# Modulation of two adaptive-norm layers: row sums of products on VectorE, in place of matmuls with the condition as weights

## The chip, the cores and the metric

The kernel runs on one core of a Trainium2 chip. The metric is the device time of one execution in microseconds (us). TensorE does the matrix products and writes them to PSUM, VectorE (DVE) and ScalarE (ACT) do the elementwise work, GpSimd (POOL) some small steps, and SyncE (SP) issues the DMA transfers.

## The reference, cut to what matters

Two blocks are computed in float32 on 256 tokens of 1024 features, beside a context of 256 tokens in the first block. The first block has two layers; each is a SwiGLU (inner width 2816), a token mixer and a second SwiGLU. Every norm is modulated, and the modulation comes from a condition vector: c for the tokens, c_ctx for the context. The second block (retention, windowed and axial attention, two MLPs) has no modulation.

```python
def _modulation(cond, w, b):                 # w: [1024, 9 * 1024]
    m = jax.nn.silu(cond) @ w + b
    return [m[:, None, j * D_MODEL:(j + 1) * D_MODEL] for j in range(N_MOD)]

def _modulate(x, g, shift, scale):
    return _rmsnorm(x, g) * (1 + scale) + shift

ml = _modulation(c, w_ada[l], b_ada[l])
mc = _modulation(c_ctx[None], w_ada[l], b_ada[l])
lat = lat + 0.5 * ml[2] * _swiglu(_modulate(lat, norm_ffn1_g[l], ml[0], ml[1]), *ffn1)
cx = cx + 0.5 * mc[2] * _swiglu(_modulate(cx, norm_ffn1_g[l], mc[0], mc[1]), *ffn1)
...                                          # mixer with parts 3 to 5, second SwiGLU with 6 to 8
```

So a layer has 9 x 1024 modulation values for each of two conditions: 72 tiles of 128 features, and 1024 products to a value.

## The kernel before, in words

Activations are kept with features as partitions and 512 tokens (256 in the later part) as columns. The weights stream from DRAM in chunks of 128x1024 float32. ScalarE rounds each to float32r (`hi`, line 145), VectorE subtracts to get the rest (`lo`, line 156), and `mm3` (lines 311 to 313) does three matmuls per tile: hi with the activation's high part, hi with its low part, lo with the high part. There are four `raw`, six `hi` and five `lo` buffers; `take` fixes the chunk in use, and `ahead_hi` and `ahead_lo` split chunks up to four or five further on.

A SwiGLU (`ffn`) goes in three thirds of 8, 7 and 7 tiles of the inner width. For each tile it takes two up chunks (w1, w3), and `gated` makes the tile g from their results: silu on ScalarE, a product on VectorE (line 550), rounding on ScalarE (552), the rest on VectorE (553). Then come eight down chunks (w2) over the third's tiles, each followed by `update` (line 434), which adds the result to x with the gate. At the last third's end `tail` does the norm, and with it the next four chunks. Results lie in six PSUM buffers (`mm`).

The order is written out by hand. Each product is a `step`: the product, then the epilogue of the step before, then `ahead_hi`, then `tick`, which advances the side work by one, then `ahead_lo`. Engines work through their queues in this order. The modulation is such side work. Its first two parts, for the first norm, are done at the program's start (`ada_pair`, line 1059) from an array of their own. The rest is the generator `ada`: columns of w_ada in units of 2048 (the last of a layer has 1024), and for a unit one tick per k, of eight. A tick loads a tile of w_ada (128 rows, 2048 columns, 1 MB, on SP's queue, three tiles ahead) and does eight matmuls (`ada_product`, line 245: four column groups, each of which the profile shows as two instructions) with the condition as weights, padded to 32 columns. After the eighth, `ada_out` transposes on VectorE (line 255), adds the bias and forms 1 + scale times the norm's gain. Layer 0's units 1 to 4 go beside its first SwiGLU, layer 1's units 0 to 3 beside layer 0's second SwiGLU. Layer 1's last unit is loaded inside its mixer (lines 609 and 1002) and put into `fill`: its products are issued by `fill_in` between the parts of the norm ahead of layer 1's second SwiGLU.

Of the kernel before, what the change touches and what calls it, by code (L numbers as in the profile page):

```python
# [26 lines left out]
def plan():  # L27
    """Weight chunks in the order of their use: (array, layer, first row, row tiles, first column, columns)."""
# [79 lines left out]
class Pair:  # L108
    """Two float32r parts, indexed as one tile [128, 2, columns]."""
# [8 lines left out]
class Weights:  # L118
    """Streams the chunks: DRAM -> float32 -> an exact pair of float32r parts (hi + lo)."""
# [60 lines left out]
def build(tc, T):  # L180
# [4 lines left out]
    with ExitStack() as ctx, tc.manual_schedule():  # L185
# [13 lines left out]
        def tmp(n=512, dt=F32):  # L199
            return tp.tile([128, n], dt, tag="t", name="t")  # L200
# [42 lines left out]
        def ada_product(ps, t, n, k):  # L243
            for g in range(4):
                nc.tensor.matmul(  # L245
                    ps[32 * g:32 * g + 32, :n // 4].rearrange("p (a b) -> p a b", b=32),
                    cond[:, k, :],
                    t[:, :n].rearrange("p (a g b) -> p a g b", g=4, b=32)[:, :, g, :],
                    start=(k == 0), stop=(k == 7), tile_position=(0, 32 * g))

        def ada_out(l, u, ps):
            """The modulation's columns from the four groups of their products."""
            nt = 16 if u < 4 else 8
            tr = tmp()
            nc.vector.transpose(out=tr[:, :nt * 32], in_=ps[:, :nt * 32])
            a = u * 16
            nc.vector.tensor_tensor(
                out=mods[l][:, a:a + nt, :], in0=tr[:, :nt * 32].rearrange("p (a b) -> p a b", b=32)[:, :, 0:2],
                in1=V(f"bada{l}")[:, a:a + nt].unsqueeze(2).to_broadcast([128, nt, 2]), op=ALU.add)
            n0, n1 = modn[l], 2 * u + nt // 8  # L260
            for j in range(n0, n1):
                sl = mods[l][:, j * 8:(j + 1) * 8, :]
                i, r = divmod(j, 3)
                if r == 1:
                    nc.vector.scalar_tensor_tensor(
                        out=scl[l][i], in0=sl, scalar=1.0,
                        in1=V(f"g_{gname[i]}{l}").unsqueeze(2).to_broadcast([128, 8, 2]),
                        op0=ALU.add, op1=ALU.mult)
                elif r == 2 and i != 1:
                    nc.vector.tensor_scalar(sl, sl, 0.5, None, ALU.mult)  # L270
            modn[l] = n1

        def ada(units, adap, lead):
            """Columns of the modulation, 2048 at a time, in four column groups of the tensor engine."""
            todo = [(l, u, k) for l, u in units for k in range(8)]
            width = lambda u: 2048 if u < 4 else 1024
            tiles = []

            def load():
                if todo:  # L280
                    l, u, k = todo.pop(0)
                    t = adap.tile([128, 2048], F32, tag="ada", name="ada")
                    n = width(u)
                    nc.sync.dma_start(out=t[:, :n], in_=T["w_ada"][l, k * 128:(k + 1) * 128, u * 2048:u * 2048 + n])
                    tiles.append(t)
            for _ in range(3):
                load()
            for _ in range(lead):
                yield 0
            first = True  # L290
            for l, u in units:
                n = width(u)
                ps = mm_ps()
                for k in range(8):
                    if not first:
                        load()
                    first = False
                    t = tiles.pop(0)
                    ada_product(ps, t, n, k)
                    yield 0  # L300
                ada_out(l, u, ps)
# [13 lines left out]
        def mmA(ps, w, X, nk, t0, t1, k0=0, k1=None, first=True):  # L315
            """Feature-major: out[n, token] += w[k, n] X[k, token]."""
# [14 lines left out]
        def step(fn, epi=None, rate=3, parts=1):  # L331
            """A product (whole or in equal parts), the epilogue of the one before, weights ahead, side work."""
# [19 lines left out]
        def rsqrt(out, in_, n, psum=False):  # L352
            """(in / n + eps) ** -0.5."""
# [14 lines left out]
        def square(o, t0, t1, later=False):  # L368
            """A tile's squares, added to the others' (later: at the next call of add_squares)."""
# [10 lines left out]
        def stats(sq, nb, n, direct=True):  # L380
            """1 / rms by token, from the squares [128 features, nb * 128 tokens] (summed): a column by block."""
# [14 lines left out]
        def bcast(r, nb):  # L396
            """By token -> the same in every partition."""
# [52 lines left out]
        fill = []  # L450

        def fill_in(n):
            """Products that nothing waits for, where the next ones wait for a norm."""
            for _ in range(min(n, len(fill))):
                fill.pop(0)()

        def norm_group(l, i, halves, more=()):
            """x is complete (its squares are in acc): norm, then the next four chunks' products."""
            new_h()
            fill_in(4)  # L460
            dgs = [stats([acc[:, t0:t1], *[s[:, t0:t1] for s in more]], 2, DM) for t0, t1 in halves]
            fill_in(2)
            ws, ps = group_start()
            for half, dg in zip(halves, dgs):
                rb = bcast(dg, 2)
                fill_in(2)
# [8 lines left out]
        def tail(l, i, nk, X, cur, nl, ni, nxt):  # L475
            """The last two tiles of a product that updates x, the norm after it and the next four chunks."""
# [65 lines left out]
        def ffn(l, i, halves, ps4, gp, end, xepi=None):  # L542
# [15 lines left out]
            epis.append(lambda: fill_in(1))  # L558
# [34 lines left out]
        def mix(l, ps4, mp, end):  # L593
# [11 lines left out]
            last_ada = None  # L605
            if l:
                last_ada = [mp.tile([128, 1024], F32, tag=f"ada{k}", name="ada") for k in range(4)]
                for k in range(4):
                    nc.sync.dma_start(out=last_ada[k], in_=T["w_ada"][l, k * 128:(k + 1) * 128, 8192:9216])
# [19 lines left out]
            def heads_view(a, hh):  # L629
                """One head of [2 sequences, 2 heads, 256 tokens]."""  # L630
# [21 lines left out]
            def hg(g, Wt):  # L652
# [9 lines left out]
                if l:  # L662
                    # The keys' factor 1 - lb is carried by the queries. Only the last state of the context is needed.
# [177 lines left out]
            def to_Y(k):  # L841
                """An operand of the out product; the first ones in the place of the first heads' forget gates."""
# [32 lines left out]
            def mmB(p, ws, b):  # L875
                """Token-major: out[token, n] += X[k, token] w[k, n], 256 columns, one block of tokens."""
# [8 lines left out]
            def gmlp(p2, b0, vg):  # L885
                """Two blocks of two groups of the gate's input: norm, then the product over the block's tokens."""
# [89 lines left out]
            # out product  # L976
# [21 lines left out]
            if l:  # L998
                for k in range(4, 8):
                    if k % 2 == 0:  # L1000
                        t = mp.tile([128, 2, 1024], F32, tag=("vt", "FR1")[k // 2 - 2], name="ada")
                    nc.sync.dma_start(out=t[:, k % 2, :], in_=T["w_ada"][l, k * 128:(k + 1) * 128, 8192:9216])
                    last_ada.append(t[:, k % 2, :])
                psa = mm_ps()
                for k in range(8):
                    fill.append(lambda k=k: ada_product(psa, last_ada[k], 1024, k))
                fill.append(lambda: ada_out(l, 4, psa))
# [17 lines left out]
        # ================= first block =================  # L1025
        H2 = [LAT, CTX]
        with ExitStack() as ph:
# [23 lines left out]
            def ada_pair(p, between=None):  # L1051
                """The first norm's shift and scale, for two tiles of features."""
# [88 lines left out]
            bg = ada([(0, 1), (0, 2), (0, 3), (0, 4)], adap, 2)  # L1141
# [4 lines left out]
        def ffn_phase(l, i, halves, ps4, units, end):  # L1146
            with ExitStack() as ph:
                gp = ph.enter_context(tc.tile_pool(name="gp", bufs=9))
                if units:
                    adap = ph.enter_context(tc.tile_pool(name="adap", bufs=3))  # L1150

                    bg = ada(units, adap, 2)
# [12 lines left out]
        r = ffn_phase(0, 2, H2, r, [(1, u) for u in range(4)], lambda nk, X: tail(0, 2, nk, X, H2, 1, 0, H2))  # L1165
        r = ffn_phase(1, 0, H2, r, [], lambda nk, X: tail(1, 0, nk, X, H2, 1, 1, H2))
        r = mix_phase(1, r)
        # ================= second block =================
# [12 lines left out]
        def scaled(o, g, late=False):  # L1181
            """x times a gain by feature, as the next product takes it (late: the second part is left to the caller)."""
# [50 lines left out]
        def proj(epi, mid=None):  # L1233
            """256 columns of a token-major product; epi takes each block of 128 tokens."""
# [15 lines left out]
        def head_scale(p, b, o=None):  # L1250
            """A block of two heads: the token's norm times that of each head."""
# [16 lines left out]
        def rope(z, cc, sn, hw, zp):  # L1268
            """z cos + swap(z) sin; the tables hold the signs."""
# [14 lines left out]
        def to_T(zs, perm, aux=False):  # L1284
            """Two blocks of two heads, token-major -> PSUM [feature, head, token]."""
# [6 lines left out]
        class Attn:  # L1292
            """Attention by head, a head at a tick: scores and softmax, then its division, transposes and values."""
# [102 lines left out]
        def x_part(p, o, g):  # L1396
            """A tile of x, what the next product takes of it and its squares; the second parts a tile later."""
# [7 lines left out]
        def mlp(l, after):  # L1405
            """x += relu(h w_up)^2 w_down, the norm of h applied to the first product's result."""
# [530 lines left out]
```

## Time and profile before

| | us |
|---|---|
| median of 3 runs | 2492.29 (2492.18 to 2492.61) |
| span of the profiled execution, first to last instruction | 2491.4 |
| TensorE busy | 2466.2 (99%) |
| VectorE busy | 1258.2 (51%) |
| ScalarE busy | 1007.1 (40%) |
| GpSimd busy | 58.7 (2%) |

The profiled execution is one of its own, and its time is known as its span; the runs' times include what lies around the span. Durations are those that the profiler reports, and one matmul's duration overlaps the next one's start, so the pace of matmuls is read from their starts. A busy share is a mean over stages that differ.

### The profile page before, as it was taken

The page shows a single profiled execution, that of the slowest core. Times are in us where ns is not written, and L with a number is a line of the kernel's source. Part 1 is how long each engine was busy: PE and PEld are TensorE (multiplying, and loading weights), DVE is VectorE, ACT ScalarE, POOL GpSimd, SP SyncE. Part 2 cuts the span into 40 slices and gives each one's busy share as a digit, 9 for nine tenths or more (in the row PEclk, how much of TensorE's full clock was granted, in tenths as well). Part 3 has the DMA queues.
Part 4 walks back from the last instruction along what each step waited for, and adds up shares of the span by engine and source line. Part 5 has one row for each costly group of instructions (what it writes and reads, how often), then busy time and mean ns, then how long its engine had stood idle before and what let it go on. Part 6 is the DMA issues. An engine that isn't in the chain of part 4 may idle for free.

```text
span 2491.4 us, 38254 instructions
## 1 busy us (share of the span) xinstructions
PE 2466.2 (99%) x15816; PEld 2148.3 (86%) x15816; DVE 1258.2 (51%) x2004; ACT 1007.1 (40%) x1646; POOL 58.7 (2%) x102
## 2 busy tenths in 40 slices
PE   7999999999999999999999999999999999999999
PEld 5666788989886667888888889989999999999999
DVE  6333334657462223344333347666566667557753
ACT  4212222537342122234222235554456556546652
POOL 0000000001000000000000000000002000001000
PEclk9999999999999999999999999999999999999999
DMA  8665322221246663223222223346556355554553
GB/s 316 241 234 184 112 98 81 84 77 60 75 147 232 235 231 112 88 82 110 94 89 98 88 82 135 111 147 201 186 171 213 111 194 188 192 163 136 189 194 126
DMA packets 99294, 367.76 MB, mean 148 GB/s; under 512 B 10920, under 2 KB 17064, under 8 KB 91952
## 3 DMA queue, kind: packets, MB, share of 16 engines
q1 hardware_dynamic: 99120, 365.32, 43.0%
q8 instruction: 124, 2.03, 0.3%
q14 instruction: 50, 0.41, 0.0%
HBM read 364.21 MB, written 1.06 MB: 147 GB/s over the span
## 4 chain that ended last, share of the span: by engine, by line
PE 91%; DVE 3%; issue 3%; ACT 2%; DMA 0%; POOL 0%; POOLq 0%; SPq 0%; DVEq 0%; ACTq 0%
PE mm L311 26%; PE mm L312 25%; PE mm L313 25%; PE mm L245 2%; PE mm L687 2%; PE mm L1230 1%; PE mm L1229 1%; PE mm L1231 1%; DVE lo L156 1%; PE mm L881 1%; PE mm L882 1%; PE mm L883 1%; ACT hi L145 1%; PE aux L400 0%; PE mm L1326 0%
## 5 line engine op out<-in xcount | busy, mean ns | idle before, releaser
L311 PE MATMUL mm<-h,hi 128*128 128x512 f32 (+1 forms) x2460 | 837.6, 340 | 2.3 <-ACT h L427 1.2
L313 PE MATMUL mm<-h,lo 128*128 128x512 f32 (+1 forms) x2460 | 828.1, 337 | 0.4 <-DVE lo L156 0.2
L145 ACT ACTIVATE hi<-raw 128x1024 fp32r<-128x1024 f32 (+1 forms) x544 | 562.9, 1041 | 580.2 <-PE mm L312 357.5
L156 DVE TENSOR_TENSOR lo<-raw,hi 128x1024 fp32r<-128x1024 f32 (+1 forms) x544 | 652.3, 1204 | 268.0 <-issue 181.9
L312 PE MATMUL mm<-l,hi 128*128 128x512 f32 (+1 forms) x2076 | 720.9, 347 | 1.2 <-DVE l L1116 0.2
L311 PEld LDWEIGHTS mm<-h,hi 128*128 128x128 f32 x2460 | 463.2, 188 | 89.8 <-ACT hi L145 15.1
L313 PEld LDWEIGHTS mm<-h,lo 128*128 128x128 f32 x2460 | 463.2, 188 | 55.2 <-DVE lo L156 1.2
L312 PEld LDWEIGHTS mm<-l,hi 128*128 128x128 f32 x2076 | 391.0, 188 | 54.2 <-DVE l L428 2.8
L311 PE MATMUL mm<-g,hi 128*128 128x256 f32 (+1 forms) x1258 | 410.9, 327 | 0.0
L313 PE MATMUL mm<-g,lo 128*128 128x256 f32 (+1 forms) x1258 | 408.6, 325 | 0.0
L312 PE MATMUL mm<-g,hi 128*128 128x256 f32 (+1 forms) x1258 | 408.6, 325 | 0.0
L311 PEld LDWEIGHTS mm<-g,hi 128*128 128x128 f32 x1258 | 236.7, 188 | 36.0 <-issue 8.8
L313 PEld LDWEIGHTS mm<-g,lo 128*128 128x128 f32 x1258 | 236.7, 188 | 22.1
L312 PEld LDWEIGHTS mm<-g,hi 128*128 128x128 f32 x1258 | 236.7, 188 | 21.4
L550 DVE TENSOR_TENSOR t<-t,mm 128x512 f32<-128x512 f32 (+1 forms) x88 | 54.6, 621 | 320.9 <-PE mm L313 319.3
L434 DVE SCALAR_TENSOR_TENSOR xT<-mm,mods,xT 128x256 f32<-128x256 f32 x192 | 86.1, 480 | 258.2 <-PE mm L313 258.0
L552 ACT ACTIVATE g<-t 128x512 fp32r<-128x512 f32 (+1 forms) x88 | 51.0, 579 | 375.8 <-DVE t L550 375.8
L312 PE MATMUL mm<-h,hi 128*128 128x256 f32 x512 | 143.8, 281 | 0.0
L1229 PE MATMUL mm<-hi,h 128*128 128x256 f32 x384 | 111.1, 289 | 0.0
L1230 PE MATMUL mm<-lo,h 128*128 128x256 f32 x384 | 107.4, 280 | 0.1
L1231 PE MATMUL mm<-hi,h 128*128 128x256 f32 x384 | 107.3, 279 | 0.0
L312 PEld LDWEIGHTS mm<-h,hi 128*128 128x128 f32 x512 | 96.5, 188 | 0.0
(296 smaller groups left out, 2370.5 us busy)
## 6 DMA issues: line engine op xcount, KB each, us to landing
raw<-wflat SPq DMA_DIRECT2D x480, 512.0 KB, 3.4
ada<-w_ada SPq DMA_DIRECT2D x56, 1024.0 KB, 4.8
raw<-wflat SPq DMA_DIRECT2D x64, 448.0 KB, 3.3
ada<-ada SPq DMA_DIRECT2D x16, 512.0 KB, 10.0
ada<-w_ada SPq DMA_DIRECT2D x16, 512.0 KB, 4.0
xT<-xT SPq DMA_DIRECT2D x2, 1024.0 KB, 6.3
bias<-d SPq DMA_DIRECT2D x2, 1024.0 KB, 7.0
out<-t SPq DMA_DIRECT2D x8, 128.0 KB, 2.7
```

What stands on the lines that cost most here:

```text
L145: self.nc.scalar.activation(out=t[:, :c], in_=self.raw[j][:, :c], func=AF.Copy)
L156: self.nc.vector.tensor_tensor(out=t[:, :c], in0=self.raw.pop(j)[:, :c], in1=w[:, 0, :c].bitcast(F32), op=ALU.subtract)
L245: nc.tensor.matmul(ps[32 * g:32 * g + 32, :n // 4].rearrange("p (a b) -> p a b", b=32), cond[:, k, :], t[:, :n].rearrange("p (a g b) -> p ...
L311: nc.tensor.matmul(out, whi, xhi, start=start, stop=False)
L312: nc.tensor.matmul(out, whi, xlo, start=False, stop=False)
L313: nc.tensor.matmul(out, wlo, xhi, start=False, stop=stop)
L434: nc.vector.scalar_tensor_tensor(out=xT[:, o, t0:t1], in0=ps[:, t0:t1], scalar=gate(l, i, o, 0 if t0 == 0 else 1), in1=xT[:, o, t0:t1], op ...
L550: nc.vector.tensor_tensor(out=m[:, :t1], in0=s[:, :t1], in1=pb[:, :t1], op=ALU.mult)
L552: nc.scalar.activation(out=t[:, 0, :t1], in_=m[:, :t1], func=AF.Copy)
L1229: nc.tensor.matmul(p[:, :256], xhi, whi, start=(k == 0), stop=False)
L1230: nc.tensor.matmul(p[:, :256], xhi, wlo, start=False, stop=False)
L1231: nc.tensor.matmul(p[:, :256], xlo, whi, start=False, stop=(k == 7))
```

## The change

w_ada is laid out in DRAM with features as rows: tile j of layer l is 128 features by the 1024 inputs, 512 KB. The condition is broadcast to all partitions, 2 x 1024 values, and silu is taken there. For each tile and each of the two conditions one VectorE instruction multiplies the tile by the condition, sums along the row, starts the sum at the bias and writes the sum to the tile's column of `mods`. One tick does one tile. 56 tiles of layer 0 (16 to 71) go beside its first SwiGLU, layer 1's tiles 0 to 39 beside layer 0's second SwiGLU, and 40 to 71 beside layer 1's first, where there was no such work. The first two parts of layer 0 (`ada_pair`) stay on TensorE. `fill`, its loads and its PSUM tile are gone, and the comments too.

```diff
-        def ada_product(ps, t, n, k):
-            for g in range(4):
-                nc.tensor.matmul(
-                    ps[32 * g:32 * g + 32, :n // 4].rearrange("p (a b) -> p a b", b=32),
-                    cond[:, k, :],
-                    t[:, :n].rearrange("p (a g b) -> p a g b", g=4, b=32)[:, :, g, :],
-                    start=(k == 0), stop=(k == 7), tile_position=(0, 32 * g))
-        def ada_out(l, u, ps):
...
+        def ada_done(l, n1):
+            for j in range(modn[l], n1):
...
+        def ada(l, t0, t1, adap, lead):
+            todo, tiles = list(range(t0, t1)), []
             def load():
                 if todo:
+                    t = adap.tile([128, 1024], F32, tag="ada", name="ada")
+                    nc.sync.dma_start(out=t, in_=T["adaT"][l, todo.pop(0)])
                     tiles.append(t)
             for _ in range(3):
                 load()
+            condb = adap.tile([128, 2, 1024], F32, tag="condb", name="condb", bufs=1)
+            nc.sync.dma_start(out=condb, in_=T["condb"].to_broadcast([128, 2, 1024]))
             for _ in range(lead):
                 yield 0
+            nc.scalar.activation(out=condb, in_=condb, func=AF.Silu)
+            for j in range(t0, t1):
+                if j > t0:
+                    load()
+                t = tiles.pop(0)
+                for c in range(2):
+                    jk = adap.tile([128, 1024], F32, tag="jk", name="jk", bufs=1)
+                    nc.vector.tensor_tensor_reduce(
+                        out=jk, in0=t, in1=condb[:, c, :], scale=1.0, scalar=V(f"bada{l}")[:, j:j + 1],
+                        op0=ALU.mult, op1=ALU.add, accum_out=mods[l][:, j, c:c + 1])
+                yield 0
+                if j % 8 == 7:
+                    ada_done(l, (j + 1) // 8)
...
         def norm_group(l, i, halves, more=()):
             new_h()
-            fill_in(4)
             dgs = [stats([acc[:, t0:t1], *[s[:, t0:t1] for s in more]], 2, DM) for t0, t1 in halves]
-            fill_in(2)
             ws, ps = group_start()
             for half, dg in zip(halves, dgs):
                 rb = bcast(dg, 2)
-                fill_in(2)
...
-            bg = ada([(0, 1), (0, 2), (0, 3), (0, 4)], adap, 2)
+            bg = ada(0, 16, 72, adap, 2)
...
-        r = ffn_phase(0, 2, H2, r, [(1, u) for u in range(4)], lambda nk, X: tail(0, 2, nk, X, H2, 1, 0, H2))
-        r = ffn_phase(1, 0, H2, r, [], lambda nk, X: tail(1, 0, nk, X, H2, 1, 1, H2))
+        r = ffn_phase(0, 2, H2, r, (1, 0, 40), lambda nk, X: tail(0, 2, nk, X, H2, 1, 0, H2))
+        r = ffn_phase(1, 0, H2, r, (1, 40, 72), lambda nk, X: tail(1, 0, nk, X, H2, 1, 1, H2))
...
-    T["w_ada"] = a["w_ada"]
+    T["adaT"] = np.ascontiguousarray(a["w_ada"].transpose(0, 2, 1)).reshape(2, 72, 128, 1024)
+    T["condb"] = np.stack([a["c"][0], a["c_ctx"]])[None]
```

VectorE's queue in the first SwiGLU's up products, before: `lo` is a weight chunk's rest, `t` and `g` the gate of a tile.

```order
L156 TENSOR_TENSOR lo<-raw,hi 128x1024 x2
L550 TENSOR_TENSOR t<-t,mm 128x512
L553 TENSOR_TENSOR g<-t,g 128x512
L156 TENSOR_TENSOR lo<-raw,hi 128x1024 x2
L550 TENSOR_TENSOR t<-t,mm 128x512
L553 TENSOR_TENSOR g<-t,g 128x512
```

The same place now; the ISA rows with `jk` are the multiply-and-reduce (`ada` the tile, `condb` the condition, `vec` the bias), those without it the read of the accumulator.

```order
L526 TENSOR_TENSOR g<-t,g 128x512
L279 ISA jk,mods_94<-ada,condb,vec 128x1024
L279 ISA mods_94 128x1
L279 ISA jk,mods_94<-ada,condb,vec 128x1024
L279 ISA mods_94 128x1
L156 TENSOR_TENSOR lo<-raw,hi 128x1024
L279 ISA jk,mods_94<-ada,condb,vec 128x1024
L279 ISA mods_94 128x1
L279 ISA jk,mods_94<-ada,condb,vec 128x1024
L279 ISA mods_94 128x1
L156 TENSOR_TENSOR lo<-raw,hi 128x1024
L523 TENSOR_TENSOR t<-t,mm 128x512
```

Between one gate's last step and the next gate's first there were two lo; now each has a tile's two reductions ahead of it.

TensorE's queue in the norm ahead of layer 1's second SwiGLU, before: `ones` are the weights of the sums of squares, `ident,r` the broadcast, and `ada` the filling products.

```order
L313 MATMUL mm<-h_12386,lo 128x256
L245 MATMUL mm<-ada,cond 32x256 x16
L386 MATMUL aux<-ones,acc 128x1
L386 MATMUL aux<-ones,t 128x1 x2
L386 MATMUL aux<-ones,acc 128x1
L386 MATMUL aux<-ones,t 128x1 x2
L245 MATMUL mm<-ada,cond 32x256 x8
L400 MATMUL aux<-ident,r 128x128 x2
L245 MATMUL mm<-ada,cond 32x256 x8
L311 MATMUL mm<-h_12598,hi 128x256
```

And now:

```order
L369 MATMUL aux<-ones,acc 128x1
L369 MATMUL aux<-ones,t 128x1 x2
L369 MATMUL aux<-ones,acc 128x1
L369 MATMUL aux<-ones,t 128x1 x2
L383 MATMUL aux<-ident,r 128x128 x2
```

The sums and the broadcast now follow each other with nothing between them.

## Rows read from the trace of the kernel before

**Rows 1.** The page's part 1: busy us, share of the span, instructions.

```profile
PE 2466.2 (99%) x15816; PEld 2148.3 (86%) x15816; DVE 1258.2 (51%) x2004; ACT 1007.1 (40%) x1646; POOL 58.7 (2%) x102
```

**Rows 2.** The chain that ended last, shares of the span by line.

```profile
by line: PE mm L311 25.5%; PE mm L312 25.1%; PE mm L313 25.1%; issue 3.1%; PE mm L245 2.5%; PE mm L687 1.5%; PE mm L1230 1.5%; PE mm L1229 1.5%; PE mm L1231 1.5%; DVE lo L156 1.0%; PE mm L881 0.8%; PE mm L882 0.8%; PE mm L883 0.8%; ACT hi L
```

**Rows 3.** Window over layer 0's first SwiGLU: us, busy by engine, clock, DMA.

```profile
51.00:403.00 352.00, 352.00 (x1617) 257.96 (x1616) 117.35 (x152) 85.49 (x106) 0.00 (x0) 1.00 0.49 172
```

**Rows 4.** Timeline of TensorE around two visits: start us, us, engine, line.

```profile
70.83 0.40 PE L313 MATMUL mm<-h,lo 128*128 128x512 f32 x1
...
72.16 0.50 PE L311 MATMUL mm<-h,hi 128*128 128x512 f32 x1
...
233.87 0.40 PE L313 MATMUL mm<-h,lo 128*128 128x512 f32 x1
...
234.77 0.50 PE L311 MATMUL mm<-h,hi 128*128 128x512 f32 x1
```

**Rows 5.** Groups by form on TensorE, line 245: count, busy us, mean ns.

```profile
L245 PE MATMUL mm<-ada,cond 128*32 128x512 f32 x448 | 59.7, 605 | 0.0
...
L245 PE MATMUL mm<-ada,cond 128*32 128x256 f32 x128 | 9.2, 387 | 0.0
```

**Rows 6.** Timeline in the norm with the filling products, three engines.

```profile
1665.46 1.93 PE L245 MATMUL mm<-ada,cond 128*32 128x256 f32 x32
1667.32 0.38 PE L386 MATMUL aux<-ones,acc 128*128 128x1 f32 x2
...
1666.15 0.42 ACT L483 ACTIVATE t<-xT 128x256 f32<-128x256 f32 x1 [2.41 <-DVE xT L434]
...
1669.31 2.34 DVE L156 TENSOR_TENSOR lo<-raw,hi 128x1024 fp32r<-128x1024 f32 x2
1671.57 0.87 DVE L419 SCALAR_TENSOR_TENSOR t<-xT,scl,aux 128x256 f32<-128x256 f32 x2
```

**Rows 7.** Groups by form on VectorE: busy us, mean ns, idle before.

```profile
L156 DVE TENSOR_TENSOR lo<-raw,hi 128x1024 fp32r<-128x1024 f32 x480 | 582.7, 1220 | 231.7 <-issue 146.0 <-PE mm L313 55.3 <-ACT hi L145 30.4
...
L156 DVE TENSOR_TENSOR lo<-raw,hi 128x896 fp32r<-128x896 f32 x64 | 69.5, 1086 | 36.3 <-issue 36.0 <-ACT hi L145 0.4
...
L428 DVE SCALAR_TENSOR_TENSOR l<-t,mods,h 128x256 fp32r<-128x256 f32 x72 | 34.3, 481 | 6.4 <-ACT h L427 6.4
...
L1333 DVE CUSTOM_DVE_ANT_0 pt<-mm,bias,sink 128x256 f32<-128x256 f32 x16 | 7.1, 479 | 3.7 <-PE mm L1326 3.7
```

**Rows 8.** Timeline of VectorE at line 1333.

```profile
1916.22 0.48 DVE L1333 CUSTOM_DVE_ANT_0 pt<-mm,bias,sink 128x256 f32<-128x256 f32 x1 [2.46 <-PE mm L1326]
1916.63 0.08 DVE L1333 DVE_READ_ACCUMULATOR2_ANT mx<- 128x1 f32 x1
```

**Rows 9.** Timeline of VectorE in up and down products without modulation; idle in brackets.

```profile
352.51 0.69 DVE L550 TENSOR_TENSOR t<-t,mm 128x512 f32<-128x512 f32 x1 [4.39 <-PE mm L313]
353.89 0.69 DVE L553 TENSOR_TENSOR g<-t,g 128x512 fp32r<-128x512 f32 x1 [0.70 <-ACT g L552]
...
358.10 1.23 DVE L156 TENSOR_TENSOR lo<-raw,hi 128x1024 fp32r<-128x1024 f32 x1 [2.37 <-issue]
363.71 0.69 DVE L550 TENSOR_TENSOR t<-t,mm 128x512 f32<-128x512 f32 x1 [4.39 <-PE mm L313]
...
304.14 0.88 DVE L434 SCALAR_TENSOR_TENSOR xT<-mm,mods,xT 128x256 f32<-128x256 f32 x2 [2.89 <-PE mm L313]
309.04 0.88 DVE L434 SCALAR_TENSOR_TENSOR xT<-mm,mods,xT 128x256 f32<-128x256 f32 x2 [2.89 <-PE mm L313]
```

**Rows 10.** DMA issues: KB each, median us to landing.

```profile
ada<-w_ada SPq DMA_DIRECT2D x16, 512.0 KB, 4.0
```

**Rows 11.** Groups by form on ScalarE.

```profile
L145 ACT ACTIVATE hi<-raw 128x1024 fp32r<-128x1024 f32 x480 | 502.4, 1054 | 489.5 <-PE mm L312 328.0 <-issue 119.1 <-DMA raw<-wflat 28.9
```

**Rows 12.** Timeline of TensorE near the program's start.

```profile
24.89 0.63 PE L312 MATMUL mm<-l,hi 128*128 128x512 f32 x1
25.31 0.63 PE L313 MATMUL mm<-h,lo 128*128 128x512 f32 x1
```

More of the change, by code (lines that the diff above doesn't have):

```diff
@@ L241, in build @@
         modn = [0, 0]
-        def ada_product(ps, t, n, k):
-            for g in range(4):
-                nc.tensor.matmul(
-                    ps[32 * g:32 * g + 32, :n // 4].rearrange("p (a b) -> p a b", b=32),
-                    cond[:, k, :],
-                    t[:, :n].rearrange("p (a g b) -> p a g b", g=4, b=32)[:, :, g, :],
-                    start=(k == 0), stop=(k == 7), tile_position=(0, 32 * g))
-        def ada_out(l, u, ps):
[L253 to L261, printed above, removed]
+        def ada_done(l, n1):
+            for j in range(modn[l], n1):
                 sl = mods[l][:, j * 8:(j + 1) * 8, :]
@@ L271, in ada_out @@
             modn[l] = n1
[L273 to L277, printed above, removed]
+        def ada(l, t0, t1, adap, lead):
+            todo, tiles = list(range(t0, t1)), []
             def load():
                 if todo:
[L281 to L284, printed above, removed]
+                    t = adap.tile([128, 1024], F32, tag="ada", name="ada")
+                    nc.sync.dma_start(out=t, in_=T["adaT"][l, todo.pop(0)])
                     tiles.append(t)
@@ L287, in ada @@
                 load()
+            condb = adap.tile([128, 2, 1024], F32, tag="condb", name="condb", bufs=1)
+            nc.sync.dma_start(out=condb, in_=T["condb"].to_broadcast([128, 2, 1024]))
             for _ in range(lead):
                 yield 0
[L290 to L301, printed above, removed]
+            nc.scalar.activation(out=condb, in_=condb, func=AF.Silu)
[11 more added lines that the diff above has]
+                    ada_done(l, (j + 1) // 8)
         def shift(l, i, k, c):
@@ L448, in group_part @@
                     mmA(ps[c], ws[c], X, 8, half[0], half[1], k, k + 1)
[L450 to L455, printed above, removed]
         def norm_group(l, i, halves, more=()):
             new_h()
-            fill_in(4)
             dgs = [stats([acc[:, t0:t1], *[s[:, t0:t1] for s in more]], 2, DM) for t0, t1 in halves]
-            fill_in(2)
             ws, ps = group_start()
@@ L557, in ffn @@
             epis.append(lambda: (gated(0, ps4[0], ps4[1]), gated(1, ps4[2], ps4[3])))
-            epis.append(lambda: fill_in(1))
             for ti, (j0, nj) in enumerate(THIRDS):
@@ L604, in mix @@
             yb = mp.tile([128, 4, t1], F32, tag="yb", name="yb")
-            last_ada = None
             if l:
-                last_ada = [mp.tile([128, 1024], F32, tag=f"ada{k}", name="ada") for k in range(4)]
-                for k in range(4):
-                    nc.sync.dma_start(out=last_ada[k], in_=T["w_ada"][l, k * 128:(k + 1) * 128, 8192:9216])
                 lb = [mp.tile([128, 2, 4], F32, tag=f"lb{d}", name=f"lb{d}") for d in range(2)]
@@ L997, in mix @@
             to_Y(7)
[L998 to L1007, printed above, removed]
             part(rest[-1:])
@@ L1150, in ffn_phase @@
                     adap = ph.enter_context(tc.tile_pool(name="adap", bufs=3))
-                    bg = ada(units, adap, 2)
+                    bg = ada(*units, adap, 2)
                     side.append(bg)
```

## The prediction

> **What bounds the kernel now.** I read the page's busy times first, then the chain that ended last, then the SwiGLU stretches in which the modulation is computed, instruction by instruction. TensorE is busy for 99% of the span, VectorE for 51% [rows 1]. Of the chain of waits 2.5% is line 245, the products that the change removes [rows 2]: they lie on the path that sets the end. A window over the first SwiGLU of layer 0 says the same: in 352 us TensorE has no idle time at all, while VectorE is busy for 117 us and ScalarE for 85 [rows 3]. What leaves TensorE here shortens the run, as long as VectorE, which gets the work, doesn't become the late one.
>
> **What leaves TensorE.** One k step of a 2048-column unit is 8 matmuls in four column groups, a visit. The last ordinary product ahead of one starts at 70.83 and the first behind it at 72.16 us, 1.33 us apart [rows 4], where ordinary products start 0.233 us apart (a down product of 21 takes 309.04 - 304.14 = 4.90 us [rows 9]): the visit costs 1.10 us. 448 such matmuls [rows 5] are 56 visits: 61.4 us. A visit of a 1024-column unit goes from 233.87 to 234.77 us [rows 4], 0.90 - 0.233 = 0.67 us. Of its 128 matmuls [rows 5], 64 are eight visits in layer 0: 5.3 us. Together 66.7 us, all in stretches where TensorE has no idle time.
>
> The other 64 stand in the norm ahead of layer 1's second SwiGLU, where TensorE waits anyway. The first 32 run from 1665.46 us, and the norm's sums start behind them at 1667.32, though the squares that they read are done at 1666.15 + 0.42 = 1666.57 us [rows 6]: without the 32 the sums start some 0.7 us earlier. What is late next: on VectorE two lo subtractions, 2.34 us, stand between the norm's reciprocal and the scaled tiles [rows 6]; they move 0.7 us forward and keep their length. So 0.7 us come off there and not the 4 us that the matmuls took. Layer 1's eight loads of w_ada inside the mixer go as well; no TensorE wait hangs on them, and I count 0.
>
> **What VectorE gets.** 56 + 40 + 32 = 128 tiles of 128 features with two multiply-and-reduce instructions of 128x1024 each, 256 in all, each followed by a read of the accumulator. The kernel before has this family at line 1333, with 256 columns and one source in PSUM: 479 ns [rows 7]. For a further column I take the lo subtraction: 1220 ns for 1024 and 1086 for 896 [rows 7], 1.05 ns a column. One instruction is then 479 + 768 x 1.05 = 1285 ns. At line 1333 the read, 0.08 us, starts 0.41 us after an instruction of 0.48 [rows 8], so a start overlaps the end before it by 0.07. A tile thus takes between 2 x 1.21 = 2.4 and 2 x (1.285 + 0.08) = 2.7 us. Both instructions write one scratch tile, so the second waits for the first; I take 2.7.
>
> Is there room? In the up products a pair of chunks takes 11.2 us (352.51 to 363.71), of which VectorE idles 0.70 + 2.37 + 4.39 us [rows 9]. The 0.70 is ScalarE's rounding between two steps of the gate and stays; 6.76 are usable, and two tiles need 5.4. In a down product of 7 tiles a chunk takes 4.90 us, 2.89 of them idle [rows 9], and a tile needs 2.7; one of 8 tiles takes 24 x 0.233 = 5.6 us and leaves 3.6. It fits everywhere, in the 7-tile downs only just. A lag of some tenths is covered there, since weights are split four chunks ahead and a late update of x only holds one of six PSUM buffers. The reductions stand ahead of lo in VectorE's queue, so lo comes 2.7 us later within a chunk, for a use four chunks (some 20 us) later. And SP's load of the next tile waits for a reduction that VectorE does ahead of the lo for which the weight load behind it on that queue waits anyway: no new wait.
>
> The sharpest place is the end of a third. The first down product's last tile needs the last gate, whose chain is 0.69 + 0.70 + 0.69 us [rows 9] from the last up product, and TensorE gets to it after 18 x 0.233 = 4.2 us. VectorE reaches the gate with 6.76 - 5.4 = 1.4 us to spare. There are seven ends in the stretches that still have reductions; 0 to 2 us each, and I take 0.5 us for all.
>
> **A page against this change.** Line 428 reads two float32 sources from SBUF and takes 481 ns for 128x256; line 1333, fused and with one source in PSUM, takes 479 [rows 7]: no difference. The Trainium skill, "Vector Engine (DVE) Microarchitecture Reference", section "Points that are easy to get wrong", says that the scalar-tensor-tensor form with two SBUF sources that aren't bf16 runs at half throughput, because no port is left for reading the accumulator back. The trace contradicts it for the plain form; the accumulating form with both sources in SBUF is in no run here. By that rule a tile would take some 4.8 us, and the change would lose (below).
>
> **Loads and ScalarE.** The tiles move the same 64 MB, in loads of 512 KB, which land in 4.0 us [rows 10] and are issued two steps, 10 us, ahead. A broadcast of the condition, 1 MB, comes three times; the DMA engines are at half their time [rows 3]. Silu of that broadcast, 128x2048, is at most 2 x 1054 ns by the hi rounding of 1024 columns [rows 11], three times, on a ScalarE that is busy for a quarter of the stretch. All of it lies beside TensorE's products: 0. Without that cover it would be 6 us.
>
> **Sum.** 61.4 + 5.3 + 0.7 = 67.4 us off, 0.5 on. The profiled span is 2491.4 us, 0.9 below the median of the runs, and what lies around it doesn't change: 2492.3 - 66.9 = 2425.4, so 2425.5. Its own range is 2422 to 2429.
>
> **Rivals.**
> *Half-rate reductions.* If the accumulating form takes two cycles a column with both sources in SBUF, an instruction is 0.48 - 256 x 0.00105 + 1024 x 0.0021 = 2.36 us and a tile 4.8. VectorE then sets the pace: 9.6 - 6.8 = 2.8 us more per pair of up chunks, 1.2 per 8-tile and 1.9 per 7-tile down. The 56 tiles of the first stretch fall on 19 pairs, 8 and 10 downs (53 + 10 + 19 = 82 us), the 40 of the second on 12 pairs, 8 and 8 (59), the 32 of the third on 12 pairs and 8 (44): 185 us, less some 10 per stretch that the lead of weights and buffers hides, 155. With 67 saved the time is 2580, slower than before. The balance turns at about 2.05 us an instruction (43 pairs at 1.4 us, 24 and 18 downs at 0.5 and 1.2, are 97 us, which less 30 is what TensorE saves). For it: the row at hand has its source in PSUM. Against: line 428, and that line 1333 costs no more than its plain relative.
>
> *A tighter fit.* At 1.5 to 1.7 us an instruction (waits between the two, no overlap) the 18 7-tile downs fall behind by up to 0.5 us and the seven ends of thirds stall by up to 2.5: 8 to 27 us come back, 2433 to 2453.
>
> *The clock in the emptied norm.* Without line 245 TensorE has only small products from 1665.5 to some 1672 us. At the program's start, between waits, its 512-column products are 0.42 us apart (24.89, 25.31 [rows 12]), the pace of 1.2 GHz against 2.4 for 0.233. If it falls so again for some 5 us, half of them are lost: 2428. The Trainium skill, "TensorE: Matmul & The Clock Gate", Part 1, has the throttled clock as the default that activity lifts; the start agrees, and no row shows a norm without filling.
>
> *The products cost nothing before.* Then it stays at 2492. The gaps of rows 4 speak against it.
>
> **Chances.** Forecast 70%, clock 10%, tighter fit 10%, half rate 9%, nothing gained 1%. The range 2421 to 2440 takes in the first two and a third of the third. A measurement can tell about 0.2%, 5 us, from no change: faster 0.90, within 0.01, slower 0.09.
>
> **What would show it.** Right: TensorE's products 0.233 us apart from step to step; 256 reductions of 1.2 to 1.3 us; VectorE at three quarters in the first stretch and still waiting for TensorE ahead of each gate. Wrong: reductions near 2.4 us; TensorE waiting for g or lo, at the ends of thirds above all; products behind the emptied norm further apart than 0.12 us for 256 columns.

## The result, and the profile after

The changed kernel takes 2420.68 us (median of 4 runs, 2420.03 to 2421.72) against 2492.23 us: ratio 0.9714, 95% interval 0.97 to 0.9728. That is 71.6 us less, where 67 were forecast, and 0.3 us below the range. The profiled span went from 2491.4 to 2419.9 us.

The page's busy times, to set beside [rows 1]:

```profile
PE 2392.5 (99%) x15240; PEld 2145.0 (89%) x15240; DVE 1565.7 (65%) x2498; ACT 1013.0 (42%) x1649; POOL 58.5 (2%) x102
```

576 matmuls are gone from TensorE and 73.7 us of its busy time; VectorE has 307.5 us more. The new instructions, as a group by form (busy us, mean ns, idle before):

```profile
L279 DVE CUSTOM_DVE_ANT_0 jk<-ada,condb,vec 128x1024 f32<-128x1024 f32 x256 | 328.1, 1282 | 11.7 <-ACT condb L272 7.2
```

1282 ns were forecast as 1285 from the 256-column instruction and the lo subtraction of [rows 7]. The window of [rows 3] over the first SwiGLU, now:

```profile
51.00:403.00 352.00, 351.87 (x1555) 285.29 (x1553) 269.57 (x399) 98.03 (x124) 0.00 (x0) 1.00 0.52 184
```

VectorE went from 117 to 270 us of 352, and TensorE still has only 0.13 us without work. How it fits shows in VectorE's timeline, in a pair of up chunks with two tiles of modulation, and then in two 7-tile down chunks with one each; [rows 9] is the same without them:

```profile
340.04 0.69 DVE L523 TENSOR_TENSOR t<-t,mm 128x512 f32<-128x512 f32 x1 [1.69 <-PE mm L296]
341.42 0.69 DVE L526 TENSOR_TENSOR g<-t,g 128x512 fp32r<-128x512 f32 x1 [0.70 <-ACT g L525]
342.03 1.28 DVE L279 CUSTOM_DVE_ANT_0 jk<-ada,condb,vec 128x1024 f32<-128x1024 f32 x1
343.24 0.08 DVE L279 DVE_READ_ACCUMULATOR2_ANT mods<- 128x1 f32 x1
343.36 1.28 DVE L279 CUSTOM_DVE_ANT_0 jk<-ada,condb,vec 128x1024 f32<-128x1024 f32 x1
344.57 0.08 DVE L279 DVE_READ_ACCUMULATOR2_ANT mods<- 128x1 f32 x1
344.57 1.09 DVE L156 TENSOR_TENSOR lo<-raw,hi 128x896 fp32r<-128x896 f32 x1
...
351.24 0.69 DVE L523 TENSOR_TENSOR t<-t,mm 128x512 f32<-128x512 f32 x1 [2.04 <-PE mm L296]
...
274.17 0.88 DVE L417 SCALAR_TENSOR_TENSOR xT<-mm,mods,xT 128x256 f32<-128x256 f32 x2 [0.36 <-PE mm L296]
...
279.07 0.88 DVE L417 SCALAR_TENSOR_TENSOR xT<-mm,mods,xT 128x256 f32<-128x256 f32 x2 [0.36 <-PE mm L296]
```

A tile takes 344.57 - 342.03 = 2.54 us. Ahead of each gate VectorE still waits 1.7 to 2.0 us for TensorE, in the 7-tile downs 0.36: every period is still TensorE's, 11.2 and 4.90 us.

Once line 245 is taken out, TensorE's products stand in the same order in both traces, 15240 of them, so the difference of each product's start is a running account of the gain (zero at the first product; positive is time saved):

| stretch (time in the trace before) | what changes there | gain in it, us |
|---|---|---|
| 11.8 to 50 us | nothing (pace at the start) | 0.2 |
| first SwiGLU, layer 0: 32 visits gone | 24 wide, 8 narrow | 34.8 |
| second SwiGLU, layer 0: 32 visits gone | 32 wide | 38.2 |
| first SwiGLU, layer 1: 32 tiles of reductions come | | 0.0 |
| norm ahead of layer 1's second SwiGLU: filling gone | | -1.8 |
| rest | nothing | 0.3 |

Two numbers differ from the prediction: the visits gave 73.0 and not 66.7 us, and the emptied norm cost 1.8 where it was to give 0.7. Where the 64 visits' further 6.3 us lay shows in the kernel before, in the rows ahead of and behind the visit of [rows 4] (PEld is the load of weights):

```profile
70.37 0.40 PE L311 MATMUL mm<-h,hi 128*128 128x512 f32 x1
70.37 0.19 PEld L312 LDWEIGHTS mm<-l,hi 128*128 128x128 f32 x1
...
72.15 0.19 PEld L311 LDWEIGHTS mm<-h,hi 128*128 128x128 f32 x1 [0.84 <-ACT hi L145]
...
72.26 0.19 PEld L312 LDWEIGHTS mm<-l,hi 128*128 128x128 f32 x1
...
72.49 0.40 PE L312 MATMUL mm<-l,hi 128*128 128x512 f32 x1
```

The first ordinary product is listed at 72.16, but its weights are loaded from 72.15 only, and the next one comes at 72.49: 0.33 us and not 0.233. In the steady pace a load lies under the product before it and starts with it (70.37); here the second load starts 0.10 us behind the first product's start (72.26), and the second product is late by as much. Behind all 64 visits the second product comes 0.335 to 0.340 us after the first and the third 0.23 us after the second. So a visit costs 1.19 us, or 0.77 if narrow: 56 x 1.19 + 8 x 0.77 = 72.8. That the load is the reason is read from these rows; the price itself is tested below.

The norm, TensorE's timeline and windows of the granted clock (the column ahead of the DMA share; 1.00 is 2.4 GHz), to set beside [rows 6]:

```profile
1592.18 0.28 PE L296 MATMUL mm<-h,lo 128*128 128x256 f32 x1
1593.46 0.35 PE L369 MATMUL aux<-ones,acc 128*128 128x1 f32 x2 [1.00 <-DVE acc L358]
...
1595.64 1.19 PE L383 MATMUL aux<-ident,r 128*128 128x128 f32 x4 [0.71 <-DVE r L374]
1598.74 0.58 PE L294 MATMUL mm<-h,hi 128*128 128x256 f32 x1 [1.91 <-ACT h L410]
...
1599.85 0.41 PE L294 MATMUL mm<-h,hi 128*128 128x256 f32 x1
1600.06 0.41 PE L295 MATMUL mm<-l,hi 128*128 128x256 f32 x1
...
1605.29 0.28 PE L296 MATMUL mm<-h,lo 128*128 128x256 f32 x1
1605.40 0.28 PE L294 MATMUL mm<-h,hi 128*128 128x256 f32 x1
```

```profile
1590.00:1595.00 5.00, 3.93 (x33) 3.67 (x32) 0.97 (x3) 0.86 (x3) 0.00 (x0) 0.99 0.28 97
1595.00:1600.00 5.00, 2.45 (x8) 1.96 (x9) 4.48 (x9) 2.45 (x5) 0.00 (x0) 0.50 0.44 138
1600.00:1605.00 5.00, 5.00 (x26) 5.00 (x25) 4.41 (x11) 3.61 (x8) 0.00 (x0) 0.50 0.18 71
```

In the kernel before, the last product ahead of the norm is this one:

```profile
1665.25 0.28 PE L313 MATMUL mm<-h,lo 128*128 128x256 f32 x1
```

There the sums start 2.07 us behind it (1667.32 [rows 6]), now 1.28 us (1592.18 to 1593.46): 0.8 us earlier, as forecast. But from 1595 the granted clock is 0.50, that is 1.2 GHz, after waits of 1.00 and 0.71 us with only small products between; the 256-column products then start 0.213 us apart, until they are back at 0.118 from 1605. Some 26 of them lose 0.095 us each, 2.5 us.

### The profile page after: what moved, and what is told of

Read it like the earlier page. It is cut to its first block, busy times and chain, and to the rows that moved or that the text cites. A ratio compares the mean times of both kernels' runs of the same rounds, so it can differ in the third digit from the quotient of the medians.

```text
span 2419.9 us, 37688 instructions
## 1 busy us (share of the span) xinstructions
PE 2392.5 (99%) x15240; PEld 2145.0 (89%) x15240; DVE 1565.7 (65%) x2498; ACT 1013.0 (42%) x1649; POOL 58.5 (2%) x102
## 4 chain that ended last, share of the span: by engine, by line
PE 91%; DVE 3%; issue 3%; ACT 2%; DMA 0%; POOL 0%; POOLq 0%; SPq 0%; DVEq 0%; ACTq 0%
PE mm L295 26%; PE mm L296 26%; PE mm L294 26%; PE mm L655 2%; PE mm L1188 2%; PE mm L1189 2%; PE mm L1187 2%; DVE lo L156 1%; PE mm L850 1%; PE mm L849 1%; PE mm L851 1%; ACT hi L145 0%; PE aux L383 0%; PE mm L1284 0%; PE aux L369 0%
## 5 line engine op out<-in xcount | busy, mean ns | idle before, releaser
L294 PEld LDWEIGHTS mm<-h,hi 128*128 128x128 f32 x2460 | 465.0, 189 | 56.7 <-ACT h L410 2.2
L279 DVE CUSTOM_DVE_ANT_0 jk<-ada,condb,vec 128x1024 f32<-128x1024 f32 x256 | 328.1, 1282 | 11.7 <-ACT condb L272 7.2
```

Of the source, the lines that this page charges most:

```text
L279: nc.vector.tensor_tensor_reduce(out=jk, in0=t, in1=condb[:, c, :], scale=1.0, scalar=V(f"bada{l}")[:, j:j + 1], op0=ALU.mult, op1=ALU.add ...
L294: nc.tensor.matmul(out, whi, xhi, start=start, stop=False)
```

## The experiments

**What a visit costs.** In the kernel before, only the last of a unit's eight k steps is multiplied:

```diff
-                    ada_product(ps, t, n, k)
+                    if k == 7:
+                        ada_product(ps, t, n, k, True)      # start=True
```

> The kernel before with one visit of TensorE per modulation unit instead of eight (only the last k step's products; the loads stay): 49 wide and 7 narrow visits fewer, VectorE's work as before. Theory (the first ordinary product behind a visit also starts its successor 0.10 us late, because its weight load isn't hidden, so a visit costs 1.20 or 0.77 us): 49 x 1.20 + 7 x 0.77 = 64 us less, 2428. Rival (a visit costs 1.10 or 0.67 us as predicted, and the rest of the gain came from the loads or queues that the change also altered): 49 x 1.10 + 7 x 0.67 = 58.6 us less, 2433.6. This leaves most of the modulation's sum out.

Measured: 2428.62 us (2427.75 to 2429.30), span 2427.4, which is 64.0 us less than 2491.4. VectorE, the loads and the queues are those of the kernel before, so the 1.19 us are the visit's own, and the rival falls.

**Fixed part or columns.** In the kernel before, two k steps to a tick:

```diff
                     ada_product(ps, t, n, k)
-                    yield 0
+                    if k % 2:
+                        yield 0
```

> The kernel before with two k steps to a tick (four tiles loaded ahead instead of three): 32 visits of 16 matmuls instead of 64 of 8, the same products in all. Theory (of a visit's 1.20 or 0.77 us, 0.43 goes with each 256 columns per group, and 0.34 is fixed: 0.24 at the switch, 0.10 for the weight load behind it): 32 x 0.34 = 10.9 us less, 2481.3. Rival (all of a visit's time goes with its columns, and the fixed part is only an extrapolation): no change.

Measured: 2481.69 us against 2492.25 us for the kernel before beside it, ratio 0.9957 (0.9941 to 0.9974): 10.6 us less, 0.33 for each of the 32 visits that went. "No change" falls. (The profiled spans, of different chips, are 11.7 us apart.) A visit of 16, on TensorE's timeline:

```profile
70.67 0.40 PE L314 MATMUL mm<-h,lo 128*128 128x512 f32 x1
71.00 1.92 PE L245 MATMUL mm<-ada,cond 128*32 128x512 f32 x16
72.85 0.50 PE L312 MATMUL mm<-h,hi 128*128 128x512 f32 x1
73.19 0.39 PE L313 MATMUL mm<-l,hi 128*128 128x512 f32 x1
```

From 70.67 to 72.85 it is 2.18 us where two separate ones take 2 x 1.33 less a product of 0.233, 2.43, and the late second product (72.85 to 73.19) comes once and not twice: 0.25 + 0.10 us, within the rows' rounding of 0.33. So 0.33 of a visit's 1.19 us, or 0.77, is the switch to it and back and doesn't go with its columns.

**Is VectorE's new work hidden?** The changed kernel with its reductions cut to 8 columns:

```diff
-                        out=jk, in0=t, in1=condb[:, c, :], scale=1.0, ...
+                        out=jk[:, :8], in0=t[:, :8], in1=condb[:, c, :8], scale=1.0, ...
```

> The changed kernel with each reduction over 8 columns instead of 1024; loads, order and number of instructions stay, VectorE has some 275 us less to do. Theory (the reductions lie wholly beside TensorE's products): the span is that of the changed kernel, 2419.9, within 0.3 us. Rival (they hold TensorE up somewhere by some tenths at the ends of thirds, as the half microsecond of the prediction has it, or more): 0.5 to 3 us less. This leaves most of the modulation's sum out.

Measured: 2420.69 us (2419.77 to 2421.80), no difference; the span, 2418.3, is 1.6 us shorter. The running account against the changed kernel places this: 0.64 us come between 26.9 and 28.1 us, ahead of the first reduction, where the pace at the start rises a little earlier, and the rest behind 1590 us, in the norm with the lower clock and later. From 60 to 1400 us, over all 256 reductions (70 to 1253 us), it changes by 0.01 us. So they cost nothing, and the span alone, against the expectation of 0.3 us, would have misled.

**How far is it from costing something?** Three and four reductions to a tile:

```diff
-                for c in range(2):
+                for c in (0, 1, 0):          # or (0, 1, 0, 1)
```

> The changed kernel with three reductions to a tile, some 3.85 us of VectorE. Theory (same usable idle times): 43 pairs at 7.7 - 6.76, 24 downs at 0.25 and 18 at 0.96 are 64 us, less up to 30 that the lead hides: 2455 to 2484. Rival (much more is hidden): within 10 us of the changed kernel, 2420 to 2431.

> The changed kernel with each of the two reductions of a tile done twice, so a tile takes some 5.1 us of VectorE, as at half rate. Theory (the usable idle time of the prediction: 6.76 us in a pair of up chunks, 3.6 in an 8-tile and 2.89 in a 7-tile down chunk): 43 pairs at 10.2 - 6.76, 24 downs at 1.5 and 18 at 2.2 are 224 us, less some 30 hidden by the lead: about 2615. Rival (the lead of four weight chunks and six PSUM buffers hides far more, since the mean use of VectorE in the stretch stays near 100%): under 2520.

Measured: 2471.19 us (ratio 0.9913, 0.9896 to 0.9929) and 2630.74 us (1.0553, 1.0538 to 1.0569); the spans are 50.6 and 208.7 us longer than with two. The account by usable idle time was 64 and 224 us with nothing hidden, 34 and 194 with 30 us hidden; what the spans grew by is 13 and 15 us below the first two. Both rivals fall. TensorE's waits, of three and then of four (us, times, longest):

```profile
PE mm L294 <- ACT g L525: 33.7, 7, 9.5
```

```profile
PE mm L294 <- ACT g L525: 110.9, 14, 13.3
PE mm L296 <- DVE lo L156: 52.4, 36, 2.5
```

VectorE's lag builds up in the up chunks and is paid at the ends of thirds, seven of them with three reductions, up to 9.5 us at a time, where a down product needs the last gate. With four, two such waits stand at each of the seven ends, and lo is late too. The mean granted clock is 0.989 with three and 0.968 with four. Set product by product against the changed kernel, products that start without a wait while the clock is 0.50 lose 14.9 us of the 50.6 and 31.7 of the 208.7. How long the waits would be without that is not shown, since VectorE catches up meanwhile.

**The emptied norm.** The changed kernel again, and with products that nobody reads in the norm, in the places of before (4, 2, 2 k steps) or later (2, 2, 4); the last also takes the next weights ahead of the sums. `fill_in(n)` stands for n k steps of products of `vec` with `cond` into a PSUM tile of their own; the three edits are shown as one, shortened:

```diff
             new_h()
+            fill_in(4)                           # late: 2
+            ws, ps = group_start()               # late_take: here
             dgs = [stats([acc[:, t0:t1], *[s[:, t0:t1] for s in more]], 2, DM) for t0, t1 in halves]
+            fill_in(2)
             ws, ps = group_start()               # late_take: not here
             for half, dg in zip(halves, dgs):
                 rb = bcast(dg, 2)
+                fill_in(2)                       # late: 4
```

> The changed kernel unaltered, beside the next three on one chip: 2420.7, span 2419.9, with TensorE's granted clock at 0.50 from about 1595 to 1605 us if that belongs to the emptied norm, and nowhere or elsewhere if it was chance.

> The changed kernel with products that nobody reads put back into the norm ahead of layer 1's second SwiGLU, in the shapes and places of the kernel before (four, two and two k steps, the first four ahead of the sums of squares). Theory (the clock fell because TensorE was quiet): the 256-column products behind the norm start 0.12 us apart and not 0.21, which gives 2.6 us back, and the sums start 0.8 us later: 1.8 us less than the changed kernel, span 2418.1. Rival (the wait of the norm itself grew, whatever TensorE does meanwhile): the same or 0.8 us more.

> The same with only two k steps ahead of the sums, where TensorE waits 1.0 us for the squares anyway, two behind the sums and four behind the broadcast. Theory: the clock stays and the sums start on time: 2.6 us less than the changed kernel, span 2417.3. Rival: the clock falls all the same, since the work ahead of the sums is less: no gain.

> The same, and the next four weight chunks are taken ahead of the sums instead of behind them, so that the two lo subtractions (2.34 us) which stand between the reciprocal and the scaled tiles on VectorE run while VectorE waits for the sums. Theory (they are what is late last in this norm): the scaled tiles start 0.7 to 1 us earlier, span 2416.3 to 2416.6. Rival (the subtractions then push the reciprocal back by as much): no change against the one before, or up to 0.5 us more.

| kernel | median us | span us | time over the norm by the account, less that of the changed kernel, us |
|---|---|---|---|
| changed, again | 2420.71 | 2419.8 | about 0 |
| filled as before | 2420.01 | 2418.4 | -1.8 |
| filled late | 2419.14 | 2417.5 | -2.6 |
| filled late, weights taken early | 2418.94 | 2417.4 | -3.1 |

The clock fell again in the unaltered kernel (0.50 from 1595 to 1600 us, 0.53 to 1605). With the filling it stays. Over whole runs the mean granted clock is 0.998 or 0.999 in all eight runs of the changed kernel and 1.000 in all thirteen with filling. Windows of the late filling, and its first products:

```profile
1595.00:1600.00 5.00, 4.56 (x61) 2.74 (x54) 4.69 (x9) 2.38 (x5) 0.00 (x0) 1.00 0.50 147
1600.00:1605.00 5.00, 5.00 (x45) 5.00 (x44) 4.35 (x12) 3.68 (x7) 0.00 (x0) 1.00 0.17 66
```

```profile
1598.54 0.38 PE L294 MATMUL mm<-h,hi 128*128 128x256 f32 x1 [0.31 <-ACT h L410]
...
1599.40 0.28 PE L294 MATMUL mm<-h,hi 128*128 128x256 f32 x1
1599.51 0.28 PE L295 MATMUL mm<-l,hi 128*128 128x256 f32 x1
```

0.118 us apart from the third product on: the first rival (the wait itself grew) falls, and so does the second (that two k steps ahead of the sums are too few). The first two fillings give the 1.8 and 2.6 us that were expected. The last kernel moves the two lo subtractions away. VectorE with the late filling, then with the early take:

```profile
1595.12 0.17 DVE L374 RECIPROCAL r<-r 128x2 f32<-128x2 f32 x1 [2.02 <-ACT r L373]
1595.20 2.34 DVE L156 TENSOR_TENSOR lo<-raw,hi 128x1024 fp32r<-128x1024 f32 x2
1597.46 0.86 DVE L402 SCALAR_TENSOR_TENSOR t<-xT,scl,aux 128x256 f32<-128x256 f32 x2
```

```profile
1595.94 0.16 DVE L374 RECIPROCAL r<-r 128x2 f32<-128x2 f32 x1
1596.96 0.88 DVE L402 SCALAR_TENSOR_TENSOR t<-xT,scl,aux 128x256 f32<-128x256 f32 x2 [0.87 <-PE aux L383]
```

The reciprocal comes later and the scaled tiles earlier, by 0.75 us against the last product ahead of the norm, as expected, and now they wait for the broadcast product. Only 0.5 us come of it in the account, and the span is 2417.4 where 2416.3 to 2416.6 were expected, and by the trace the filling itself is now in the way:

```profile
1596.86 1.93 PE L441 MATMUL mm<-vec,cond 128*32 128x256 f32 x32
...
1598.72 0.39 PE L294 MATMUL mm<-h,hi 128*128 128x256 f32 x1
```

The first scaled tile is rounded by 1598.0 us, but TensorE is still at the four k steps that stand ahead of its product; a shorter filling there was not tried. All four medians lie within 0.1%, and the 95% intervals of their ratios overlap. The nine runs of the two late fillings (2416.82 to 2419.57 us) all lie below the eight of the changed kernel (2420.00 to 2421.72); those filled as before (2419.61 to 2420.55) don't, and for them the gain is shown only by where the traces' products start. Nor do the runs tell the two late fillings apart.

## Why the prediction was wrong, point by point

**What leaves TensorE: right mechanism, one term too small.** This is the step that took the time out of the range. The forecast price of a visit, 1.10 and 0.67 us, ended at the start of the first product behind it; the next one starts 0.10 us late, and the price is 1.19 and 0.77. The row that shows it (72.49 us) is not among those that the prediction used. It makes 6.3 us by the account (73.0 and not 66.7), and this alone takes the time below the range.

**The norm: the first half right, the second wrong.** The sums do start 0.8 us earlier, and the lo subtractions are then late, as stated. That TensorE keeps its pace there was the error: 0.7 us of gain were forecast and 1.8 of loss came. The rival on the clock was named with its place and its price (half of some 5 us; measured 1.8 + 0.8 = 2.6), and got 10%; it was the case, and the fillings in the experiments show the cause. The prediction had nothing against it but that no row showed a norm without filling, which is no evidence. The Trainium skill, "TensorE: Matmul & The Clock Gate", Part 1, has the throttled clock as the default and activity as what lifts it. The trace agrees (0.50 granted from 1595 to 1605 us, 1.00 with the fillings).

The two errors have opposite signs: 6.3 - 2.5 = 3.8, and with 0.5 us for ends of thirds that didn't stall and 0.5 at the start and behind the norm, where nothing was changed, this is the 4.8 us between 2425.5 and 2420.7. That the miss of the range is as small as 0.3 us is luck: with the pace kept in the norm it would have been some 3 us.

**What VectorE gets: right.** 1282 ns for 1285, 2.54 us a tile for 2.4 to 2.7, 270 us of 352 busy. The estimate from the family's 256-column row held, and the rival at half rate fell: an instruction would have taken 2.36 us. The Trainium skill, "Vector Engine (DVE) Microarchitecture Reference", section "Points that are easy to get wrong", states half throughput for a scalar-tensor-tensor form with two SBUF sources that aren't bf16. The trace doesn't show it for the instruction used here (1282 ns), which the profile lists as a custom one; whether that is the form the page means no run shows. The rival's price was of the right order: 155 us for 4.8 us a tile, where four reductions, 5.1 us, cost 209. (The sum at its balance point is 94 us and not 97, which changes nothing else.)

**Room and ends of thirds: right.** 6.76 and 2.89 us usable fit what three and four reductions cost; with two nothing is late, so the 0.5 us put on the ends of thirds were 0.

**Loads, SP and ScalarE: 0, right.** The broadcast lands in 9.5 us (median of three), silu takes 1.90 us, and VectorE waits for the silu three times, 7.2 us in all, without making TensorE late.

## What to carry to other kernels

Price a short foreign job on a busy TensorE from the last product ahead of it to the second one behind it, since the way back costs time too (0.10 us here); and a job that can't move is cheaper in fewer, longer pieces (two k steps to a visit gave 10.6 us, with one more tile loaded ahead). Work that fills a wait on TensorE may be worth keeping for its clock alone: ask what runs at half pace behind the wait before it is taken out. For work moved to VectorE, count idle time by kind of step, without the gaps inside a dependent chain, and look at the step in which another engine needs VectorE's last result.

## What the runs showed of the hardware that was not expected

The fused multiply-and-reduce with two float32 sources in SBUF takes 1282 ns for 1024 columns, 62 ns more than the plain subtraction of that size; its read of the accumulator, 83 ns, begins under its end. Behind each of 64 groups of eight products with 32 weight columns, the second ordinary product starts 0.10 us late. The granted clock was 1.00 through the norm with filling products, in three kernels, and 0.50 for some 10 us without them, in two runs of the same kernel; in the kernel with short sums it fell for less time (0.69 and 0.63 in the same two windows).
